# Two-layer decoder trunk: other places for the odd layer's decays, another order of its third head's projections, and other lengths in its list schedule

## The chip, the cores and the metric

The kernel runs on one core of one Trainium2 chip, as one launch. The metric is the device time of one execution in microseconds (us). An execution under the profiler gives the trace; its own time stands beside the times of runs without it.

## The reference, cut to what matters

One sequence of 1024 tokens with width 1024 goes through an even layer (windowed attention and a gated linear recurrence), an odd layer (gated DeltaNet) and a last RMSNorm. The change touches the odd layer alone, the last third of the kernel's instructions and some 1020 of its 2234 us. With 8 key heads of 128 and two value heads of 128 for each, it computes:

```python
def odd_mixer(hn, w_in, conv_w, dt_bias, a_log, norm_w, w_out):
    qkv, z, b_logit, a_logit = _split(hn @ w_in, ODD_SIZES)
    qkv = jax.nn.silu(causal_depthwise_conv(qkv, conv_w))
    q, k, v = _split(qkv, ...)          # q, k are l2-normalized
    beta = jax.nn.sigmoid(b_logit)
    g = -jnp.exp(a_log) * jax.nn.softplus(a_logit + dt_bias)
    o = gated_delta_rule_chunked(q, k, v, g, beta)
    o = rms_norm(o, norm_w) * jax.nn.silu(z)
    return o @ w_out

# gated_delta_rule_chunked, for one chunk, gcum = cumsum(g) within it
lower = where(strict, (k * beta) @ k.T * exp(gcum_i - gcum_j), 0)
u, w  = solve(I + lower, [v * beta, k * beta * exp(gcum)])
attn  = where(causal, q @ k.T * exp(gcum_i - gcum_j), 0)
v_new = u - w @ S
o     = (q * exp(gcum)) @ S + attn @ v_new
S     = S * exp(g_last) + (k * exp(g_last - gcum)).T @ v_new
```

The exponentials of differences of `gcum` are the decays: one 128 x 128 matrix for `lower` and one for `attn`, for every chunk and value head.

## The kernel before, in words

**Tiling.** The odd layer walks over the 8 key heads `hh`; both value heads (`e` = 0, 1) of a key head go together, so most tiles of the recurrence are 128 x 2 x 128. The sequence is cut into `NT` = 8 chunks `c` of 128 tokens. All projections are products of the normed input `hn` with weights in three fp32r terms (hi x hi, hi x lo, lo x hi), 128 x 512 a matmul: 8 slices of the inner dimension by 3 terms are 24 matmuls for one half of the tokens, 48 for one column group of 128. Their PSUM banks are `pj`, of which there are two (`BANKS`, L303).

**Stages for a head.** `proj(j)` (L1182) holds the column groups that are computed while an earlier head's recurrence runs: first `way_out(j - 2)` (the two groups of the gate z of head j - 2), then k of head j + 1, the two v groups and q of head j. PSUM names in the profile: `pk`, `pv`, `pq` for these, `oz` for z. `conv` (L1103) does the causal convolution and SiLU on ACT and DVE after a projection, `turn_k`, `turn_v`, `turn_q` transpose on PE. Weights come in units of two column groups: `unit` (L349) hands out the next one of `queue` (L316) and loads the one after it; each is four DMAs of 256 KB into `raww`, split by an ACT cast (hi) and a DVE subtraction (lo). The units are w41 (k0), w42 (k1, v0_0), w43 (v0_1, q0), w44 (k2, v1_0), w45 (v1_1, q1), w46 (z0), w47 (k3, v2_0), w48 (v2_1, q2) and so on.

**`invert(hh)`** (L1255) builds the inverse of I + `lower` for all 16 chunk and value-head pairs: `kk` = k k^T on PE; DVE multiplies it by beta and the decay into the big tile `L` (128 x 16 x 128, two places); then 31 steps on 32 x 32 blocks (`Lp`, `Tp`, `tm` on DVE) and small matmuls (`qp`, `up`, `q2`, `u2`) turn L into the inverse U, in the same tile. The decays come from `gcd`, a 128 x 128 array of `gcum` in DRAM that `gates()` (L1039) writes at the start of the layer: `decays` (L1249) loads two rows of it, the same for all partitions, into a small tile of 128 x 2 x 128 (128 KB of writes), and `decay_l` (L1261) runs two relus with a bias and one exponential on it. For L these tiles are `gcl` (two places, 8 loads a head), for the attention matrix `gca` (two places, 8 loads a head), which POOL masks and ACT exponentiates.

**`recur(hh)`** (L1360) is the recurrence over the chunks. A chunk is a chain between engines: `ks` = k S on PE, `r` on DVE, `vp` = U r on PE, `vt` on DVE and `vn` on ACT, `kv` = k^T vt on PE, then the new S on DVE. Beside it run `qs` (its eviction is `oq`, on ACT), `op` = A vn and `qk` for the next chunk; `attend` (L1372) multiplies `qk` with the decay into `A` (two places).

**The gate's way out.** `gate` (L1197) evicts `oz` into `g` (128 x 512, one place), for both e and both halves h: four tiles a head. `gated` multiplies the normed output by g and stores it to `ymix`; `normed` needs the whole recurrence of that head. At the end, `out_last` loads the mixed tiles back (`rawy`, cast into `oyh` and `yplo`) and the residual (`hr`, eight loads), multiplies by the output weights, adds and norms.

**What sets the order.** The code is written as generators, and `mix` and `blend` (L366, L376) interleave recurrence, inversion and projections by rough amounts of work. In the odd layer nothing is issued at once: each call is recorded by `Plan` and `run` (L203) makes a list schedule over all five engines. It simulates time with `times` (L107: how long an instruction holds its engine and when its result is there) and `SEM` (the delay of a semaphore to another engine), and takes on each engine, among the instructions that could start, the one that was recorded first. `give` (L266) then issues all in the order of the simulated starts, and each engine works strictly in that order. A tile whose place is still used waits for its old users. Since all of them go through one helper, the profile shows every instruction of the odd layer on L270 (and the even layer's on L284).

Of the kernel before, what the change touches and what calls it, by code (L numbers as in the profile page):

```python
# [10 lines left out]
F32 = mybir.dt.float32  # L11
# [70 lines left out]
class Plan:  # L82
# [7 lines left out]
    SEM = {"PE": 500, "DVE": 300, "ACT": 300, "POOL": 300, "SP": 300}  # L90

    def __init__(self):
        self.ops = None
# [13 lines left out]
    def times(self, op, last):  # L107

        key, name, a = op["key"], op["name"], op["a"]
        n = self.elems(op["out"][0])  # L110
        if key == "SP":
            return 420, 3200
        if key == "PE":
            if name == "transpose":
                return 109, 280
            r32 = a[1].dtype == F32R
            rows, cols = a[2].ap[0][1], self.elems(a[1])
            small = rows < 128 or cols < 128
            if small:
                held = 2.0 * (8 if cols == 32 else 18)  # L120
            else:
                held = n / 2.4 * (1 if r32 else 4) + (14 if r32 else 8)
            if small != last.get("small", False):
                held += 120
            last["small"] = small
            return held, held + 190
        if key == "DVE":
            if name == "transpose":
                t = 1950 if n >= 1024 else 1070 if op["out"][0].ap[-1][0] != 1 or a[1].ap[-1][0] != 1 else 620
            elif name == "memset":  # L130
                t = 60 + 0.82 * n
            elif n < 20:
                t = 85
            elif n >= 512:
                t = 100 + 1.15 * n
            else:
                t = 70 + 1.08 * n
            return t, t + 80
        if key == "ACT":
            t = 210 + 0.75 * n if n > 128 else 300  # L140
            if "accum_out" in op["kw"]:
                t = 440
            return t, t + 95
        if name == "memset":
            return 560, 600
        t = 780 if n <= 256 or a[0].ap[0][1] == 32 else 1330
        return t, t + 40
# [55 lines left out]
    def run(self):  # L203
# [42 lines left out]
        while done_n < n:  # L246
# [9 lines left out]
            i = min(i for i in ready[k] if at[i] <= s)  # L256
# [34 lines left out]
def trunk_kernel(ctx: ExitStack, tc: tile.TileContext, x, ew, ewo, ow, owab, owo, nw, fnw, lbl, hnw,  # L291
# [26 lines left out]
    for i in (21, *sorted(range(24), key=lambda i: (i // 3 + i % 3, i % 3 < 2, i) if i % 3 == 2 else (i // 3, 1, i))):  # L318
        queue += [(ow[i], 4)]
# [70 lines left out]
    def drain(fill):  # L390
        for _ in fill:
            pass
# [634 lines left out]
    def odd_layer(es):  # L1027
# [221 lines left out]
        def decays(hh, c, w):  # L1249
            g = sp.tile([P, 2, 128], F32, name=f"gc{w}{hh}_{c}", tag=f"gc{w}", bufs=2)  # L1250
# [4 lines left out]
        def invert(hh):  # L1255
# [5 lines left out]
            def decay_l(c):  # L1261
                gcB = decays(hh, c, "l")

                for e in range(2):
                    act.activation(gcB[:, e, :], gcB[:, e, :], AF.Relu, bias=gt["ngc"][:, c, 2 * hh + e:2 * hh + e + 1])
                act.activation(gcB, gcB, AF.Exp, scale=-1.0)
                return gcB

            ahead_l = [decay_l(0)]
            for h in range(2):  # L1270
# [4 lines left out]
                for c in range(4 * h, 4 * h + 4):  # L1275
                    gcB = ahead_l.pop()
                    if c < NT - 1:
                        ahead_l.append(decay_l(c + 1))
# [81 lines left out]
        def recur(hh):  # L1360
# [4 lines left out]
            def decay_a(c):  # L1365
                DA = decays(hh, c, "a")
# [5 lines left out]
            def attend(c):  # L1372
# [190 lines left out]
```

## Time and profile before

| | |
|---|---|
| median of 3 runs | 2235.93 us (2234.35 to 2236.56) |
| the profiled execution | 2235.39 us, of which its span is 2233.6 us |
| mean granted TensorE clock | 0.979 |
| HBM read, written | 151.25 MB, 29.49 MB |
| ACT / POOL busy | 947.2 us / 239.2 us |
| loads of L's decays (`gcl`) | 64 of 128 KB, 3.2 us from issue to landing |
| loads of A's decays (`gca`) | 64 of 128 KB, 3.0 us |
| loads of odd weights (`raww`) | 100 of 256 KB, 3.0 us |

Lines of operations give name and PSUM or SBUF tile as out<-in, partitions x elements, and a count; buffer numbers are left out, so `oz` is z of any head. PE is the matrix engine, PEld its weight load, DVE, ACT and POOL are the vector, scalar and GpSimd engines, SP issues the DMAs. A granted clock of 1.00 is TensorE's full speed, 0.50 half of it. The page cuts the span into 40 slices of 55.8 us with the busy tenths of each engine; the clock's row and PE's are:

```profile
PE   7999999999999999989998998899999999999998
PEclk9999999999999999989998998799999999999999
```

The 25th and 26th of them (1340 to 1452 us) are in the odd layer, where heads 0 and 1 are worked on.

### The profile page before, as it was taken

Reading aid. Unit: us, or ns where it says so; the run is one execution under the profiler, and the core shown is the slowest. Engines: PE = TensorE matmul, PEld = TensorE weight load, DVE = VectorE, ACT = ScalarE, POOL = GpSimd, SP = SyncE. Lnnn points to the kernel's source line nnn. Section 1 sums busy time; section 2 is a strip of 40 time slices with the busy share of each in tenths; the row PEclk is TensorE's granted clock in tenths of the full one; section 3 lists DMA queues with packets and bytes.
Section 4 is the critical chain, followed back from the end, with each engine's and each line's share of the span. In section 5 each row is a group of like instructions: output and inputs, shape, how many; then the busy total and the mean of one; then the engine's idle time right before and its main releaser. Section 6 shows DMA issues by size and latency. Waiting matters only on the chain. (4 is left out here: it accounts for less than half of the span.)

```text
span 2233.6 us, 52459 instructions
## 1 busy us (share of the span) xinstructions
PE 2162.9 (97%) x21781; PEld 1780.9 (80%) x21781; DVE 1393.5 (62%) x3236; ACT 947.2 (42%) x2551; POOL 239.2 (11%) x252
## 2 busy tenths in 40 slices
PE   7999999999999999989998998899999999999998
PEld 6888888888787878767786776788888888887886
DVE  6353545453444444446666798697897988865677
ACT  6233333333223222222124855657566565653223
POOL 0011111110000000000000001312212121130100
PEclk9999999999999999989998998799999999999999
DMA  4111111114333434362233212212213121224223
GB/s 149 39 49 45 48 44 49 49 39 122 84 102 93 114 104 115 92 171 88 92 100 108 87 46 55 70 48 79 79 57 83 49 83 53 83 74 150 89 95 123
DMA packets 100078, 184.14 MB, mean 82 GB/s; under 512 B 12672, under 2 KB 30208, under 8 KB 99840
## 3 DMA queue, kind: packets, MB, share of 16 engines
q1 hardware_dynamic: 99840, 180.79, 26.5%
q8 instruction: 171, 2.80, 0.5%
q14 instruction: 67, 0.55, 0.1%
HBM read 151.25 MB, written 29.49 MB: 81 GB/s over the span
## 5 line engine op out<-in xcount | busy, mean ns | idle before, releaser
L284 DVE TENSOR_TENSOR w_lo<-raww,w_hi 128x512 fp32r<-128x512 f32 x160 | 117.9, 740 | 150.0 <-ACT w_hi L284 149.5
L284 ACT CAST w_hi<-raww 128x512 fp32r<-128x512 f32 x160 | 99.4, 621 | 203.7 <-DMA raww<-in_ewo_dram 54.2
L270 PE MATMUL op<-w_hi,yplo 128*128 128x512 f32 x448 | 140.4, 392 | 0.7 <-DVE hr L270 0.6
L284 ACT ACTIVATE P<-P,nm 128x256 f32<-128x256 f32 (+7 forms) x128 | 71.4, 559 | 133.4 <-DVE nm L284 133.3
L270 ACT CAST w_hi<-raww 128x512 fp32r<-128x512 f32 x132 | 81.8, 621 | 89.8 <-DMA raww<-in_owo_dram 42.8
L270 DVE TENSOR_TENSOR hr<-hr,op 128x512 f32<-128x512 f32 x128 | 87.4, 685 | 48.7 <-PE op L270 46.2
L284 PE MATMUL op<-w_hi,yphi 128*128 128x512 f32 x320 | 105.9, 405 | 7.9 <-DVE hres L284 4.8
L270 DVE TENSOR_TENSOR w_lo<-raww,w_hi 128x512 fp32r<-128x512 f32 x132 | 96.3, 732 | 20.5 <-ACT w_hi L270 17.5
L270 PE MATMUL pv<-hn_hi,w_hi 128*128 128x512 f32 x256 | 107.4, 419 | 0.0
L270 PE MATMUL oz<-hn_hi,w_hi 128*128 128x512 f32 x256 | 107.3, 419 | 0.0
L270 PE MATMUL pv<-hn_hi,w_lo 128*128 128x512 f32 x256 | 103.6, 405 | 0.0
L270 PE MATMUL pv<-hn_lo,w_hi 128*128 128x512 f32 x256 | 102.4, 400 | 0.0
L270 PE MATMUL oz<-hn_hi,w_lo 128*128 128x512 f32 x256 | 102.2, 399 | 0.0
L270 PE MATMUL oz<-hn_lo,w_hi 128*128 128x512 f32 x256 | 101.9, 398 | 0.0
L284 DVE STREAM_TRANSPOSE PB<-P 128x256 f32<-128x256 f32 (+3 forms) x64 | 54.6, 853 | 72.9 <-ACT P L284 72.9
L270 PEld LDWEIGHTS op<-w_hi,yplo 128*128 128x128 f32 x448 | 84.1, 188 | 18.9 <-DVE hr L270 1.5
L270 POOL TENSOR_TENSOR gca<-gca,MA 128x256 f32<-128x256 f32 x64 | 54.6, 854 | 366.0 <-DMA gca<-gcd 196.3
L270 PE MATMUL op<-w_lo,yplo 128*128 128x512 f32 x224 | 86.9, 389 | 0.0
L284 DVE TENSOR_TENSOR hres<-hres,op 128x512 f32<-128x512 f32 x96 | 64.7, 682 | 31.7 <-PE op L284 30.9
L284 DVE CUSTOM_DVE_ANT_0 P<-S,G 128x256 f32<-128x256 f32 (+7 forms) x128 | 58.1, 491 | 36.8 <-PE S L284 36.5
L284 PEld LDWEIGHTS op<-w_hi,yphi 128*128 128x128 f32 x320 | 62.0, 194 | 23.8 <-DVE hres L284 5.6
L284 PE MATMUL avp<-w_hi,hn_hi 128*128 128x256 f32 x256 | 74.6, 291 | 0.0
(345 smaller groups left out, 6352.6 us busy)
## 6 DMA issues: line engine op xcount, KB each, us to landing
raww<-in_ew_dram SPq DMA_DIRECT2D x128, 256.0 KB, 3.0
raww<-in_ow_dram SPq DMA_DIRECT2D x100, 256.0 KB, 3.0
V<-vd SPq DMA_DIRECT2D x64, 256.0 KB, 5.3
rawy<-ymix SPq DMA_DIRECT2D x64, 256.0 KB, 2.7
raww<-in_ewo_dram SPq DMA_DIRECT2D x32, 256.0 KB, 3.0
gcl<-gcd SPq DMA_DIRECT2D x64, 128.0 KB, 3.2
gca<-gcd SPq DMA_DIRECT2D x64, 128.0 KB, 3.0
ymix<-oy SPq DMA_DIRECT2D x32, 256.0 KB, 2.8
```

Of the source, the lines that this page charges most:

```text
L270: ops[i]["f"](*ops[i]["a"], **ops[i]["kw"])
L284: return f(*a, **kw)
```

## The change

**Places of the decays.** `decays` no longer loads into tiles of its own. For L, `invert` loads two chunks (four matrices) at a time straight into their part of `L`, four DMAs of 256 KB a head instead of eight of 128 KB; ACT does four relus and one exponential on 512 elements there, and DVE multiplies in place. For A the load goes into a tile of tag `A`, which now has four places, and `attend` multiplies in place.

**Order.** `proj(2)`, the projections issued beside head 1's recurrence and ahead, no longer begins with the gate z of head 0: it is v2_0, then z0 with `GATE` = 8 steps of it ahead of k3, then the rest of z0, v2_1 and q2. The `queue` of weights follows: w46 is now (k3, v2_0) and w47 is z0. The gate's tile `g` has two places.

**The schedule.** Each recorded instruction gets a rank `want`, which is its number in the record, less `lead` for steps wrapped in `plan.early`: `gates()` and `invert(0)` are recorded with a lead of 10000. The list schedule takes the least `want` among what could start. `SEM` goes from 300 to 250 for four engines, an engine's wait for its own result from 0 to 40 (`OWN`), and most lengths in `times` are other numbers.

The diff, cut to its core (of the lengths two lines are shown):

```diff
-    SEM = {"PE": 500, "DVE": 300, "ACT": 300, "POOL": 300, "SP": 300}
+    SEM = {"PE": 500, "DVE": 250, "ACT": 250, "POOL": 250, "SP": 250}
+    OWN = 40
...
-        self.ops.append(dict(key=key, f=f, name=name, a=a, kw=kw, out=out, ins=ins, i=len(self.ops)))
+        self.ops.append(dict(key=key, f=f, name=name, a=a, kw=kw, out=out, ins=ins, i=len(self.ops), want=len(self.ops) - self.lead))
+    def early(self, lead, steps):
+        while True:
+            old, self.lead = self.lead, lead
+            z = next(steps, None)
+            self.lead = old
+            if z is None:
+                return
+            yield z
...
         if key == "SP":
-            return 420, 3200
+            return 430, 3100
...
-                if k is None or k == key and k not in ("PE", "SP"):
+                if k is None:
                     t = done
                 else:
-                    t = 0.0 if k == key == "PE" else done + self.SEM[k]
+                    t = 0.0 if k == key == "PE" else done + (self.OWN if k == key else self.SEM[k])
...
-            i = min(i for i in ready[k] if at[i] <= s)
+            i = min((i for i in ready[k] if at[i] <= s), key=lambda i: ops[i]["want"])
...
-    for i in (21, *sorted(range(24), key=lambda i: (i // 3 + i % 3, i % 3 < 2, i) if i % 3 == 2 else (i // 3, 1, i))):
+    for i in (21, *sorted(range(24), key=lambda i: (i // 3, 1, i) if i % 3 < 2 else (i // 3 + 2, i == 2, i + 4.5 * (i == 2)))):
...
         def proj(j):
-            if j > 1:
+            if j > 1 and j != 2:
                 yield from way_out(j - 2)
             w = unit()
             late = (lambda: turn_q(j - 1)) if j else (lambda: turn_k(0))
-            if j < 7:
-                yield from conv(w, 0, 9 + j, f"k{j + 1}", lambda: k_tile(j + 1), late)
-            yield from conv(w, 1, 16 + 2 * j, f"v{j}_0", lambda: v_tile(j, 0), (lambda: turn_k(j + 1)) if j < 7 else late)
+            k = lambda mid: conv(w, 0, 9 + j, f"k{j + 1}", lambda: k_tile(j + 1), mid)
+            v = lambda mid: conv(w, 1, 16 + 2 * j, f"v{j}_0", lambda: v_tile(j, 0), mid)
+            tk = lambda: turn_k(j + 1)
+            tv = lambda: turn_v(j, 0)
+            if j == 2:
+                yield from v(late)
+                out = way_out(0)
+                for _ in range(GATE):
+                    yield next(out)
+                yield from k(None)
+                yield from out
+                tv = lambda: (turn_v(j, 0), turn_k(j + 1))
+            elif j < 7:
+                yield from k(late)
+                yield from v(tk)
+            else:
+                yield from v(late)
             w = unit()
-            yield from conv(w, 0, 17 + 2 * j, f"v{j}_1", lambda: v_tile(j, 1), lambda: turn_v(j, 0))
+            yield from conv(w, 0, 17 + 2 * j, f"v{j}_1", lambda: v_tile(j, 1), tv)
             yield from conv(w, 1, j, f"q{j}", lambda: q_tile(j), lambda: turn_v(j, 1))
+        GATE = 8
...
-                g = G7[0][:, e, h, :] if hh == 7 else sp.tile([P, 512], F32, name=f"g{hh}_{e}_{h}", tag="g")
+                g = G7[0][:, e, h, :] if hh == 7 else sp.tile([P, 512], F32, name=f"g{hh}_{e}_{h}", tag="g", bufs=2)
...
-        def decays(hh, c, w):
-            g = sp.tile([P, 2, 128], F32, name=f"gc{w}{hh}_{c}", tag=f"gc{w}", bufs=2)
+        def decays(hh, c):
+            g = sp.tile([P, 2, 128], F32, name=f"A{hh}_{c}", tag="A", bufs=4)
...
-            def decay_l(c):
-                gcB = decays(hh, c, "l")
-                for e in range(2):
-                    act.activation(gcB[:, e, :], gcB[:, e, :], AF.Relu, bias=gt["ngc"][:, c, 2 * hh + e:2 * hh + e + 1])
-                act.activation(gcB, gcB, AF.Exp, scale=-1.0)
-                return gcB
-            ahead_l = [decay_l(0)]
+            for c in range(0, NT, 2):
+                sync.dma_start(L[:, 2 * c:2 * c + 4, :],
+                               bass.AP(tensor=gcd.tensor, offset=gcd.offset + (c * 16 + 2 * hh) * 128,
+                                       ap=[[0, P], [16 * 128, 2], [1, 256]]))
+                for u in range(4):
+                    act.activation(L[:, 2 * c + u, :], L[:, 2 * c + u, :], AF.Relu,
+                                   bias=gt["ngc"][:, c + u // 2, 2 * hh + u % 2:2 * hh + u % 2 + 1])
+                act.activation(L[:, 2 * c:2 * c + 4, :], L[:, 2 * c:2 * c + 4, :], AF.Exp, scale=-1.0)
...
                         dve.scalar_tensor_tensor(L[:, 2 * c + e, :], kk[:, c - 4 * h, :], SC[hh][:, 0, c, e:e + 1],
-                                                 gcB[:, e, :], op0=ALU.mult, op1=ALU.mult)
+                                                 L[:, 2 * c + e, :], op0=ALU.mult, op1=ALU.mult)
...
-                A = sp.tile([P, 2, 128], F32, name=f"A{hh}_{c}", tag="A", bufs=2)
-                dve.tensor_tensor(A, qk[:, None, :].to_broadcast([P, 2, 128]), DA, op=ALU.mult)
-                return A
+                dve.tensor_tensor(DA, qk[:, None, :].to_broadcast([P, 2, 128]), DA, op=ALU.mult)
+                return DA
...
-        fill = blend(gates(), start())
+        fill = blend(plan.early(10000, gates()), start())
...
-        drain(blend(invert(0), fill, 0.8))
+        drain(blend(plan.early(10000, invert(0)), fill, 0.8))
```

What that makes of the order on each engine is shown at three places. A row has the line, the operation and out<-in with the tiles' full names (the head and the chunk stand behind the letters: `ks0_5` is chunk 5 of head 0, `oz0_0_0` the first half of z0's first column group).

First PE, where head 0's recurrence is at chunk 5. Before:

```order
L270 MATMUL ks0_5_14593<-S0_4_14584,kT0_14256 128x256
L270 MATMUL qs0_5_14595<-S0_4_14584,q0_14392 128x256
L270 MATMUL vp0_5_14600<-r0_5_14594,L0_14294 128x128 x2
L270 MATMUL op0_5_14606<-vn0_5_14602,A0_5_14588 128x128
L270 MATMUL kv0_5_14604<-vt0_5_14601,kn0_14292 128x256
L270 MATMUL op0_5_14606<-vn0_5_14602,A0_5_14588 128x128
L270 MATMUL qk0_6_14608<-q0_14392,kT0_14256 128x128
L270 MATMUL ks0_6_14612<-S0_5_14605,kT0_14256 128x256
L270 MATMUL qs0_6_14614<-S0_5_14605,q0_14392 128x256
```

With the change:

```order
L291 MATMUL oz0_0_0_14675<-hn_hi0_13908,w47_hi0_14616 128x512
L291 MATMUL ks0_5_14571<-S0_4_14563,kT0_14256 128x256
L291 MATMUL qs0_5_14573<-S0_4_14563,q0_14384 128x256
L291 MATMUL oz0_0_0_14675<-hn_lo0_13910,w47_hi0_14616 128x512
L291 MATMUL oz0_0_0_14675<-hn_hi0_13908,w47_lo0_14617 128x512
L291 MATMUL oz0_0_0_14675<-hn_hi1_13909,w47_hi1_14619 128x512
L291 MATMUL oz0_0_0_14675<-hn_lo1_13911,w47_hi1_14619 128x512
L291 MATMUL oz0_0_0_14675<-hn_hi1_13909,w47_lo1_14620 128x512
L291 MATMUL oz0_0_0_14675<-hn_hi1_13909,w47_hi1_14619 128x512
L291 MATMUL oz0_0_0_14675<-hn_lo1_13911,w47_hi1_14619 128x512
L291 MATMUL oz0_0_0_14675<-hn_hi1_13909,w47_lo1_14620 128x512
L291 MATMUL vp0_5_14578<-r0_5_14572,L0_14294 128x128
```

Before, the chunks 4 to 7 of head 0 follow each other on PE with no projection between them. Now matmuls of z0 stand between the steps of a chunk, eight of them between `qs0_5` and the first `vp0_5`.

Second SP, which issues the loads, where the array `gcd` has just been written. Before:

```order
L270 DMA gcd_14213<-gcs__14227 128x128
L270 DMA gcl0_0_14296<-gcd_14213 128x256
L270 DMA gcl0_1_14298<-gcd_14213 128x256
L270 DMA gca0_0_14395<-gcd_14213 128x256
L270 DMA raww44_0_14328<-in_ow_dram 128x512
L270 DMA gca0_1_14418<-gcd_14213 128x256
L270 DMA raww44_1_14331<-in_ow_dram 128x512
L270 DMA gcl0_2_14299<-gcd_14213 128x256
L270 DMA gcl0_3_14300<-gcd_14213 128x256
```

With the change:

```order
L291 DMA gcd_14213<-gcs__14227 128x128
L291 DMA raww43_2_14268<-in_ow_dram 128x512
L291 DMA raww43_3_14271<-in_ow_dram 128x512
L291 DMA L0_14294<-gcd_14213 128x2x256 x4
L291 DMA A0_0_14387<-gcd_14213 128x256
L291 DMA L1_14388<-gcd_14213 128x2x256 x4
L291 DMA raww44_0_14320<-in_ow_dram 128x512
L291 DMA raww44_1_14323<-in_ow_dram 128x512
```

Before, single loads of decays stood among those of the weights w44. Now the eight loads of L for heads 0 and 1, with A's first between them, are in one piece ahead of w44.

Third ACT, near the end of the layer, where `rawy` is cast into `yplo` and chunk 5 of head 7 follows. Before:

```order
L270 CAST yplo1_9_16379<-rawy256_0_1_16381 128x512
L270 ACTIVATE oj7_4_0_16403,oss7_16242<-bv7_16197 128x128
L270 CAST yplo1_9_16379<-rawy256_1_0_16382 128x512
L270 ACTIVATE oj7_4_1_16404,oss7_16242<-bv7_16197 128x128
L270 CAST yplo1_9_16379<-rawy256_1_1_16383 128x512
L270 ACTIVATE oq7_5_16410<-qs7_5_16409,g_eg_14220 128x128 x2
```

With the change:

```order
L291 CAST yplo1_9_16254<-rawy256_0_1_16256 128x512
L291 ACTIVATE oj7_4_0_16277,oss7_16122<-bv7_16079 128x128
L291 ACTIVATE oj7_4_1_16278,oss7_16122<-bv7_16079 128x128
L291 CAST yplo1_9_16254<-rawy256_1_0_16257 128x512
L291 CAST yplo1_9_16254<-rawy256_1_1_16258 128x512
L291 ACTIVATE oq7_5_16284<-qs7_5_16283,g_eg_14220 128x128 x2
```

Two squares (`oj7_4`) stand in another place between the casts; `oq7_5` is behind the last cast in both.

More of the change, by code (lines that the diff above doesn't have):

```diff
@@ L119, in times @@
             if small:
-                held = 2.0 * (8 if cols == 32 else 18)
+                held = 28 if cols == 32 else 62
             else:
-                held = n / 2.4 * (1 if r32 else 4) + (14 if r32 else 8)
+                held = n / 2.4 * (1 if r32 else 4) + (17 if r32 else 8)
             if small != last.get("small", False):
-                held += 120
+                held += 100
             last["small"] = small
@@ L128, in times @@
             if name == "transpose":
-                t = 1950 if n >= 1024 else 1070 if op["out"][0].ap[-1][0] != 1 or a[1].ap[-1][0] != 1 else 620
+                t = 1980 if n >= 1024 else 1060 if out.ap[-1][0] != 1 or a[1].ap[-1][0] != 1 else 95 + 1.03 * n
             elif name == "memset":
-                t = 60 + 0.82 * n
-            elif n < 20:
-                t = 85
+                t = 60 + 0.86 * n
+            elif n < 24:
+                t = 82
+            elif out.ap[0][1] == 32:
+                t = 715
             elif n >= 512:
-                t = 100 + 1.15 * n
-            else:
-                t = 70 + 1.08 * n
-            return t, t + 80
+                t = (65 if name == "scalar_tensor_tensor" and len(op["ins"]) == 3 else 12) + 1.155 * n
+            elif name == "scalar_tensor_tensor":
+                t = 260
+            else:
+                t = 72 + 1.03 * n
+            return t, t + 83
         if key == "ACT":
[L140 to L143, printed above, removed]
+            if n < 24:
+                t = 200
+            elif op["ins"][0].space == PSUM:
+                t = 249 if n <= 128 else 268 if n <= 256 else 0.93 * n
+            else:
+                t = 293 if n <= 128 else 307 if n <= 256 else 1.02 * n
+            if n >= 512 and (len(op["ins"]) > 1 or out.ap[0][1] == 32):
+                t += 100
+            return t, t + (230 if "accum_out" in op["kw"] else 110)
         if name == "memset":
-            return 560, 600
-        t = 780 if n <= 256 or a[0].ap[0][1] == 32 else 1330
-        return t, t + 40
+            return 565, 565
+        t = 750 if n <= 256 or out.ap[0][1] == 32 else 1010 if len(op["ins"][1].ap) > 2 else 1250
+        return t, t + 50
     def edges(self):
```

14 lines of the change are left out of this document (6 added, 8 removed).

## The prediction

> **What bounds the kernel now.** I read the page first, then the busy time by stage, then what TensorE (PE) waited for, then its timeline where it waited longest.
>
> ```profile
> span 2233.6 us, 52459 instructions
> ...
> PE 2162.9 (97%) x21781; PEld 1780.9 (80%) x21781; DVE 1393.5 (62%) x3236; ACT 947.2 (42%) x2551; POOL 239.2 (11%) x252
> ```
>
> PE is busy for 97% of the span, so an edit pays only where PE idles or runs at a lower clock. The odd layer begins near 1213 us. The next rows are the busy time in stretches of it: stretch, length, then PE, PE's weight loads, DVE, ACT, POOL with instruction counts, and last the granted clock, DMA share and rate.
>
> ```profile
> 1250.00:1275.00 25.00, 21.42 (x97) 17.28 (x96) 19.60 (x58) 18.93 (x58) 2.08 (x2) 0.93 0.33 98
> 1275.00:1350.00 75.00, 73.96 (x555) 60.51 (x554) 67.95 (x172) 40.95 (x107) 5.89 (x9) 1.00 0.19 57
> 1350.00:1368.78 18.78, 18.78 (x99) 16.04 (x97) 14.61 (x36) 15.03 (x46) 2.62 (x3) 1.00 0.37 88
> 1368.78:1419.76 50.98, 38.71 (x335) 30.32 (x334) 36.27 (x124) 18.36 (x61) 13.59 (x18) 0.60 0.09 26
> 1419.76:1507.00 87.24, 85.97 (x633) 71.48 (x632) 73.65 (x214) 56.78 (x174) 13.50 (x17) 1.00 0.23 66
> 1507.00:2020.00 513.00, 512.24 (x3621) 427.95 (x3621) 417.57 (x1129) 311.28 (x943) 118.26 (x127) 1.00 0.25 72
> 2020.00:2060.00 40.00, 35.51 (x159) 29.24 (x158) 20.68 (x44) 12.77 (x37) 1.61 (x2) 0.91 0.48 172
> 1450.00:1500.00 50.00, 50.00 (x413) 41.61 (x412) 48.41 (x140) 30.05 (x87) 8.03 (x10) 1.00 0.14 41
> ```
>
> The loss sits in one place: from 1368.78 to 1419.76 PE is idle for 50.98 - 38.71 = 12.3 us and its clock is 0.60. From 1507 to 2020, heads 2 to 6, it is idle for 0.8 of 513 us at full clock: nothing is to be won there. What that stretch looks like, in PE's timeline (start, length, operation, in brackets the idle time before and who ended it), first where chunks of head 0's recurrence stand among projection matmuls, then where they stand alone:
>
> ```profile
> 1361.65 0.48 PE L270 MATMUL oz<-hn_hi,w_hi 128*128 128x512 f32 x1
> 1361.97 0.59 PE L270 MATMUL kv<-vt,kn 128*128 128x256 f32 x2
> 1362.40 0.38 PE L270 MATMUL qk<-q,kT 128*128 128x128 f32 x2
> 1362.54 0.47 PE L270 MATMUL oz<-hn_lo,w_hi 128*128 128x512 f32 x1
> ...
> 1364.24 0.60 PE L270 MATMUL ks<-S,kT 128*128 128x256 f32 x2
> 1364.67 0.59 PE L270 MATMUL qs<-S,q 128*128 128x256 f32 x2
> ...
> 1365.34 0.40 PE L270 MATMUL oz<-hn_hi,w_hi 128*128 128x512 f32 x1
> 1365.57 0.40 PE L270 MATMUL oz<-hn_lo,w_hi 128*128 128x512 f32 x1
> ```
>
> ```profile
> 1372.27 0.67 PE L270 MATMUL ks<-S,kT 128*128 128x256 f32 x2 [0.82 <-DVE tm L270]
> ...
> 1378.43 0.95 PE L270 MATMUL ks<-S,kT 128*128 128x256 f32 x2 [1.00 <-DVE S L270]
> 1379.17 1.06 PE L270 MATMUL qs<-S,q 128*128 128x256 f32 x2
> 1381.01 1.22 PE L270 MATMUL vp<-r,L 128*128 128x128 f32 x4 [0.78 <-ACT oq L270]
> 1382.75 0.80 PE L270 MATMUL op<-vn,A 128*128 128x128 f32 x2 [0.52 <-ACT vn L270]
> 1383.34 1.09 PE L270 MATMUL kv<-vt,kn 128*128 128x256 f32 x2
> ...
> 1385.42 1.19 PE L270 MATMUL ks<-S,kT 128*128 128x256 f32 x2
> ```
>
> From start to start a projection matmul takes 0.23 us (1365.34 to 1365.57), a pair on 128x256 0.43 (kv to qk, ks to qs), so a pair on 128x128 about half, 0.22. A chunk is three pairs of the first kind (ks, qs, kv) and five of the second (two vp, two op, qk): 1.29 + 1.10 = 2.4 us of PE. Alone it takes 1378.43 - 1372.27 = 6.2 us, since each step waits for DVE or ACT, and 1385.42 - 1378.43 = 7.0 us once the clock is halved. The projection that should lie between is out of work: oz of head 0 has one place for its gate g, and the place comes free only when head 0's recurrence is over and its output is normed.
>
> **The change part by part**, against the profiled execution's own 2235.39 us (span 2233.6 and 1.8 around it); the median of the three runs is 0.5 above that.
>
> *Order of the third head's projections, and two places for g.* Nothing is added or removed. In the changed PE order, from ks of chunk 3 of head 0 on, 15 to 23 matmuls of pv2, oz0 and pk3 stand between one ks and the next (91 in all), where before 16 stood in chunk 3 and none in chunks 4 to 7. A chunk needs 6.2 - 2.4 = 3.8 us of cover; 18 matmuls of 0.23 are 4.1. The cover is there, not by much. What goes is what the stretch wastes. From below: PE's busy time at the granted clock is at most 38.71 x 0.60 = 23.2 us of full-speed work, so at least 50.98 - 23.2 = 27.8 us are lost. From above: if all of it is stretched like a chunk, 2.4 of 7.0, the work is 17.5 us and 33.5 are lost. Both rows describe the same stretch, so I take the middle, **-31**.
>
> *What is late next: DVE.* From 1275 to 1507 DVE is busy for 67.95 + 14.61 + 36.27 + 73.65 = 192.5 of 232 us, and its work stays. Were it to reach the share of 1275 to 1350 (67.95 / 75 = 0.906), it would need 212.5 us, and only 19.5 could be saved; at the share of 1450 to 1500 (48.41 / 50 = 0.968) 198.8 us, and 33 could. I take what lies between, nearer the upper row because that one has PE at 50.00 of 50: 28 saved, that is **+3** on the term above.
>
> *Decays loaded into L's and A's own places.* Each head loads L in four DMAs of 256 KB instead of eight of 128 KB, with one exponential on 512 columns where two on 256 stood: 32 DMAs and 32 ACT instructions fewer. ACT and SP bound nothing (56.78 of 87.24 busy on ACT at the busiest), so I cost that at nothing; the cover is PE's own work. But in SP's changed order the loads for L of heads 0 and 1 stand in one piece, with A's first between them, ahead of the weights w44. How fast such loads run, before, is in the SP queue's timeline and the DMA rate by slices of 0.275 us from 1246 to 1257:
>
> ```profile
> 1246.89 0.80 SPq L270 DMA_DIRECT2D gcl<-gcd  x2
> 1247.74 0.43 SPq L270 DMA_DIRECT2D gca<-gcd  x1
> 1248.27 0.38 SPq L270 DMA_DIRECT2D raww<-in_ow_dram  x1
> ```
>
> ```profile
> GB/s 205 22 0 0 0 0 26 89 89 93 71 93 89 93 71 71 52 97 115 97 89 134 253 294 175 164 186 190 179 175 264 257 197 205 89 86 93 74 37 7
> ```
>
> While gcl and gca alone are in flight the rate is about 90 GB/s. At that rate a load of L takes 2.9 us, four 11.6, and all nine some 25 us: L0 is whole about 10 us after its first load, and the weights behind it land near 1270 instead of 1255. ACT and DVE take their work in order, so PSUM copies and weight splits behind L0's exponentials wait too. PE before loses there:
>
> ```profile
> PE kk L270 <- DVE L L270: 2.8, 1, 2.8
> ```
>
> That wait may go, since gates and inversion now come first (by some 2 us at PE), or be replaced by one for the copies behind L. Bounds: 3.6 us better (all of 25 - 21.42) and 9 worse (the 11.6 less the 2.8 waited now). I take **+3**, nearer the middle since the first PE work that needs w44 (pk2) stands over 20 us behind.
>
> The Trainium skill ("DMA: Bandwidth & Descriptors", Anatomy of one DMA) fits a DMA at about 2.0 us plus its bytes at 436 GB/s, for the GpSimd path; by that, an estimate, a load of L costs 2.6 us, mostly latency that overlaps, and the four land within 4 us of one another. The rate row disagrees for these loads, which read the same few rows for all partitions; by the page the last term would be nothing and the time 2207.
>
> *List schedule with new lengths.* It orders all of the layer. Where PE is at 512.24 of 513 there is nothing to win: 0, with 5 us either way as many ranks change. The stall near 2041 to 2046 stays:
>
> ```profile
> 2043.89 0.62 ACT L270 CAST yplo<-rawy 128x512 fp32r<-128x512 f32 x1 [6.83 <-DMA rawy<-ymix]
> ```
>
> The cast waits for a load that stands in SP's queue behind eight loads of the residual, and the changed order has the same eight ahead of it and the same oq behind it. Nothing of the 40 - 35.51 is won.
>
> **Sum:** -31 + 3 + 3 = -25 us: 2235.4 - 25 = **2210 us**.
>
> **Rivals.** *DVE is the bound* (chance 0.16). It gets through its work no faster than at 0.906: 19.5 saved, less 3 for L, gives 2219. For it: from 1275 to 1350 it is the fullest engine beside PE. Against it: 48.41 of 50 later on. *All of it goes* (0.13): 33 saved and the early wait gone too gives 2199. *The stall only moves* (0.04): PE's filling is used up early and PE starves later instead, from 1420 to 1507; 2235. Against it: PE would have to lose 25 us where it is now idle for 1.3, with both orders alike again from head 2's recurrence on.
>
> *Slower* (0.04): the burst of L loads in every head. Each L now has to wait for its place, then for 11.6 us of loads, and ACT, in order, holds PSUM copies behind its exponentials. PE has two banks for projections, 24 matmuls or 5.5 us each; once ACT is held for longer, PE stops. It decides from there on. A stop of the size seen at 2041 (4.5 idle, and 0.91 of the clock over 40 us adds some 3) is about 7 us; in each of seven heads that is 49, less 25: 2259. Against it is what ACT waits now between 1500 and 2000, without PE noticing:
>
> ```profile
> ACT gcl L270 <- DMA gcl<-gcd: 23.0, 17, 4.1
> ```
>
> *The clock does not come back* (0.01). The stretch has a clock of 0.60 though the idle times before its rows are 1.0 us or less; if something else halves it, only the 12.3 idle us can go: 2223. The Trainium skill ("TensorE: Matmul & The Clock Gate", HAM oscillation) gives the rule that only PE-idle gaps over about 3.4 us matter. The trace speaks against that as a rule on single gaps, since short ones in a row were enough here; and the clock is 1.00 again as soon as projections return.
>
> **How the numbers follow.** The forecast has 0.62, for 2203 to 2217: DVE's bounds, L's from -3 to +9 and the 5 us either way do not add up all in one direction. With the two neighbours the range is **2199 to 2222**, which leaves out the same, the slower and a little at both ends. A change of 0.2%, 4.5 us, is about what a measurement of this kernel can tell from none. Faster by more than that: 0.62 + 0.16 + 0.13 + 0.01 = **0.92**; the same **0.04**; slower **0.04**.
>
> **What would show it.** Right: no PE stretch with a clock of 0.6 between head 0's chunks 3 and 7; oz and pk between ks and vp there; DVE at 0.93 or more of the time from Lp0 to head 2's first chunk; the 4.5 us stop near the end unchanged. For L: loads of L0 that land about 3 us apart. Wrong: PE waits for ACT behind L's exponentials in each head, or a new stretch at half clock in heads 1 or 2.

## The result, and the profile after

The changed kernel takes 2266.55 us (median of 4 runs, 2264.51 to 2271.7) against 2235.14 of the kernel before beside it: ratio 1.0143, 95% interval 1.0125 to 1.0162. It is slower by 31 us, where 25 less were predicted. The profiled execution took 2265.53 us. First its page (span, then busy time of each engine):

```profile
span 2263.8 us, 52378 instructions
...
PE 2159.7 (95%) x21781; PEld 1777.9 (79%) x21781; DVE 1410.1 (62%) x3236; ACT 943.2 (42%) x2519; POOL 240.7 (11%) x252
```

PE does the same matmuls and is idle for 2263.8 - 2159.7 = 104.1 us, before for 70.7. Busy time by stretch of the changed kernel, with the columns and the bounds of the prediction's table:

```profile
1250.00:1275.00 25.00, 19.81 (x85) 16.04 (x84) 17.18 (x47) 18.65 (x55) 3.31 (x4) 0.86 0.46 106
1368.78:1419.76 50.98, 42.32 (x400) 34.26 (x400) 31.87 (x95) 26.96 (x76) 14.39 (x17) 0.90 0.25 48
1419.76:1507.00 87.24, 75.63 (x580) 61.68 (x579) 71.93 (x210) 50.00 (x150) 19.65 (x22) 0.94 0.31 73
1507.00:2020.00 513.00, 486.88 (x3451) 406.69 (x3451) 421.64 (x1100) 287.70 (x855) 105.90 (x115) 0.98 0.21 64
```

The stretch that was to get better did: from 1368.78 the clock is 0.90 where it was 0.60, and 8.7 us are idle, not 12.3. Head 0's chunks are covered as forecast: PE is not idle there until 1390, when L's loads for head 2 go out. The 8.7 us come behind these: 5.5 at `ot` (transposes of the output `bv`), which waits for POOL, which waits for a load of A until 1407.83, and 3.2 at `q`, which waits for a step of the inversion that stands behind the relus on ACT. At the first head, from 1250 to 1275, 5.2 us are idle where 3.6 were. The loss is where nothing had been lost: 11.6 us idle from 1419.76 (1.3 before) and 26.1 from 1507 to 2020 (0.8 before), with a clock that falls below 1. What PE waits for in the odd layer (total, times, longest):

```profile
PE kk L291 <- DVE L L291: 30.2, 12, 6.6
PE up L291 <- issue: 8.4, 1, 8.4
PE ot L291 <- POOL bv L291: 5.5, 1, 5.5
PE q L291 <- ACT L L291: 4.1, 2, 3.2
```

The first row is new in size: before it stood at 2.8 in one place. The page's part on DMA issues (count, size, median us from issue to landing) says what is behind it:

```profile
L<-gcd SPq DMA_DIRECT2D x32, 256.0 KB, 11.7
A<-gcd SPq DMA_DIRECT2D x64, 128.0 KB, 2.9
```

A load for L lands after 11.7 us; the small loads of before took 3.2, and the list schedule plans 3.1. A load of A that goes out behind such a burst is late too, up to 15.6 us where the median is 2.9. One of the stops, in head 4, by the timelines of SP, ACT, DVE and PE (in brackets the idle time before, and who ended it):

```profile
1583.46 1.92 SPq L291 DMA_DIRECT2D L<-gcd  x4
...
1589.16 0.69 ACT L291 ACTIVATE L<-L,g_ngc 128x128 f32<-128x128 f32 x2 [2.80 <-DMA L<-gcd]
...
1597.93 0.40 ACT L291 ACTIVATE L<-L,g_ngc 128x128 f32<-128x128 f32 x1 [3.58 <-DMA L<-gcd]
...
1599.05 0.61 ACT L291 ACTIVATE uq<-q 128x512 f32<-128x512 f32 x1
...
1599.70 0.69 DVE L291 SCALAR_TENSOR_TENSOR q<-uq,q 128x512 f32<-128x512 f32 x1 [4.17 <-ACT uq L291]
1600.31 0.34 DVE L291 SCALAR_TENSOR_TENSOR L<-kk,sc,L 128x128 f32<-128x128 f32 x1
...
1594.22 0.83 PE L291 MATMUL kk<-kT 128*128 128x128 f32 x6
1600.71 0.80 PE L291 MATMUL kk<-kT 128*128 128x128 f32 x2 [5.65 <-DVE L L291]
1601.15 0.77 PE L291 MATMUL oz<-hn_hi,w_hi 128*128 128x512 f32 x1
1601.73 0.63 PE L291 MATMUL oz<-hn_lo,w_hi 128*128 128x512 f32 x1
1602.15 0.63 PE L291 MATMUL oz<-hn_hi,w_lo 128*128 128x512 f32 x1
```

The four loads go out at once when L's place is free. ACT, in order, stands at a relu until the third lands (1597.93); behind it is `uq`, a step of the convolution of q. DVE waits for that, and its first multiplication into L is behind. PE waits 5.65 us for that multiplication at the last of the four products of `kk`, and then runs at half speed for some 3 us more (0.42 from start to start where 0.23 is full speed). The same chain comes back in heads 5, 6 and 7 (4.9, 6.7 and 5.1 us).

### The profile page after: what moved, and what is told of

Its sections match the earlier page's. It is cut to its first block, busy times and chain, and to the rows that moved or that the text cites. A ratio compares the mean times of both kernels' runs of the same rounds, so it can differ in the third digit from the quotient of the medians.

```text
span 2263.8 us, 52378 instructions
## 1 busy us (share of the span) xinstructions
PE 2159.7 (95%) x21781; PEld 1777.9 (79%) x21781; DVE 1410.1 (62%) x3236; ACT 943.2 (42%) x2519; POOL 240.7 (11%) x252
## 5 line engine op out<-in xcount | busy, mean ns | idle before, releaser
L291 POOL TENSOR_TENSOR A<-A,MA 128x256 f32<-128x256 f32 x64 | 53.4, 836 | 447.7 <-DMA A<-gcd 217.5
L291 DVE SCALAR_TENSOR_TENSOR vT<-uv,cws,vT 128x512 f32<-128x512 f32 x96 | 73.7, 769 | 4.6 <-ACT vT L291 2.9
## 6 DMA issues: line engine op xcount, KB each, us to landing
L<-gcd SPq DMA_DIRECT2D x32, 256.0 KB, 11.7
```

Of the source, the lines that this page charges most:

```text
L291: ops[i]["f"](*ops[i]["a"], **ops[i]["kw"])
```

## The experiments

All were measured with runs of the kernel before on the same chip (its medians there: 2232.8 to 2234.3). A table first; "rows" is the order of the decays' array in DRAM, explained below.

| kernel | loads for L | order of head 2's projections | plan | median us | ratio to before, interval |
|---|---|---|---|---|---|
| e1_small_loads | 8 small, apart | new | new | 2227.5 | 0.9973 (0.9963 to 0.9984) |
| e2_in_place_only | 4 in L | old | old | 2272.3 | 1.0169 (1.0149 to 1.0189) |
| e3_order_only | 8 small, apart | new | old | 2228.2 | 0.9974 (0.9964 to 0.9984) |
| e4_long_l_in_plan | 4 in L | new | new, L's load long | 2221.9 | 0.9941 (0.9923 to 0.9958) |
| e5_one_run_rows | 4 in L, new rows | new | new | 2213.1 | 0.9907 (0.989 to 0.9923) |
| e6_one_run_rows_plan | 4 in L, new rows | new | new, L's load measured | 2210.0 | 0.9901 (0.9886 to 0.9915) |
| e7_long_l_old_order | 4 in L | old | new, L's load long | 2225.1 | 0.9968 (0.9957 to 0.9979) |
| e8_lengths_only | 8 small, apart | old | new | 2239.9 | 1.0032 (1.002 to 1.0044) |
| e9_rows_plan_old_order | 4 in L, new rows | old | new, L's load measured | 2226.0 | 0.9966 (0.9953 to 0.9979) |
| e10_rows_in_place_only | 4 in L, new rows | old | old | 2234.6 | 1.0009 (1.0 to 1.0019) |
| e11_rows_in_place_order | 4 in L, new rows | new | old | 2226.3 | 0.9968 (0.9955 to 0.9981) |

**Which part costs: e1 to e4.** The changed kernel with the small loads back (`oy` gives up a place for their tiles):

```diff
-            for c in range(0, NT, 2):
-                sync.dma_start(L[:, 2 * c:2 * c + 4, :],
-                               bass.AP(tensor=gcd.tensor, offset=gcd.offset + (c * 16 + 2 * hh) * 128,
-                                       ap=[[0, P], [16 * 128, 2], [1, 256]]))
+            def decay_l(c):
+                gcB = decays(hh, c, "gcl", 2)
...
-            y = sp.tile([P, 512], F32, name=f"oy{hh}_{e}_{h}", tag="oy", bufs=2)
+            y = sp.tile([P, 512], F32, name=f"oy{hh}_{e}_{h}", tag="oy")
```

> The changed kernel, but the decays for L are loaded as before: eight loads of 128 KB a head into two small tiles, two ahead (the tile oy has one place instead of two, to make room). All else is the change's: the order of the third head's projections, two places for g, A in place, the new lengths. Theory 'burst' (the four loads of L at once hold the DMA engines for 15 us in each head; ACT, DVE and then PE at kk wait behind them): the stops of heads 2 to 7, some 55 us of the trace's excess, go, and 2205 to 2218 us come out, no PE wait for kk over 1 us in heads 4 to 7. Theory 'schedule' (the new lengths put kk too early on PE, however the decays are loaded): 2250 or more. Theory 'order' (the moved projections upset the later heads): 2250 or more.

2227.5: the slowdown is gone and 'schedule' and 'order' fall, but the gain is 7 us, not the 16 to 29 that 'burst' had. What PE waits for longest from 1340 to 1600 in the profiled execution, which was its slowest (2233.95 us):

```profile
PE qp L291 <- DVE ors L291: 5.0, 1, 5.0
PE qp L291 <- DVE Un L291: 2.9, 1, 2.9
```

At `kk` it waits 0.4 us at the longest there and 1.2 in the later heads. PE waits at `qp` for DVE, which ends the inversions of heads 1 and 2 too late.

The kernel before with L and A in place and nothing else:

```diff
-                gcB = decays(hh, c, "l")
...
+            for c in range(0, NT, 2):
+                sync.dma_start(L[:, 2 * c:2 * c + 4, :],
+                               bass.AP(tensor=gcd.tensor, offset=gcd.offset + (c * 16 + 2 * hh) * 128,
+                                       ap=[[0, P], [16 * 128, 2], [1, 256]]))
```

> The kernel before with one part of the change: decays loaded into L (four loads of 256 KB) and into A (four places). Order, g and lengths are those of before. Theory 'burst': stops in most heads as in the changed kernel, some 40 to 55 us, so 2270 to 2295 us, with the bare stretch of head 0 still at half clock. Theories 'schedule' and 'order': within 6 us of before.

2272.3, as 'burst' said: this part alone costs 38 us. The other theories had it at no difference; they fall. Here PE stops at other places than in the changed kernel: at `qk` for DVE's work on q, which in head 5 waits for `uq` behind a relu on ACT (13.2 us in 5 places), and at `ot` for POOL's `bv` (11.4 in 6). The order alone:

```diff
-            if j > 1:
+            if j > 1 and j != 2:
                 yield from way_out(j - 2)
...
-                g = G7[0][:, e, h, :] if hh == 7 else sp.tile([P, 512], F32, name=f"g{hh}_{e}_{h}", tag="g")
+                g = G7[0][:, e, h, :] if hh == 7 else sp.tile([P, 512], F32, name=f"g{hh}_{e}_{h}", tag="g", bufs=2)
...
-            y = sp.tile([P, 512], F32, name=f"oy{hh}_{e}_{h}", tag="oy", bufs=2)
+            y = sp.tile([P, 512], F32, name=f"oy{hh}_{e}_{h}", tag="oy")
```

> The kernel before with the other part of the change alone: the third head's projections and their weights in the new order and two places for g (oy has one place instead of two, to make room). Decays and lengths are those of before. Theory 'burst': the prediction's first two terms were right, 2206 to 2216 us, and no stretch at half clock between 1370 and 1420 us. Theory 'order': 2235 or more.

2228.2, a miss for both theories: the order gains 6 us, not 18 to 28. Its windows show where the rest went:

```profile
1350.00:1368.78 18.78, 14.80 (x81) 12.51 (x81) 12.71 (x33) 15.86 (x59) 1.74 (x2) 0.94 0.27 57
1368.78:1419.76 50.98, 50.32 (x411) 41.55 (x411) 47.20 (x135) 25.57 (x73) 14.01 (x16) 0.96 0.15 44
...
1450.00:1475.00 25.00, 22.43 (x103) 17.45 (x102) 24.71 (x84) 16.26 (x54) 2.70 (x3) 0.86 0.11 29
1475.00:1507.00 32.00, 28.88 (x291) 22.79 (x290) 26.39 (x71) 10.88 (x28) 10.79 (x13) 0.95 0.23 67
...
1507.00:1600.00 93.00, 88.73 (x668) 73.02 (x669) 77.57 (x223) 58.47 (x179) 14.51 (x17) 1.00 0.20 62
```

The old stretch is full (50.32 of 50.98). But PE now loses 4.0 us just ahead of it, where it lost none: 3.5 of them at `vp` for `oq`, on ACT, which is busy for 15.86 of 18.78. And it loses 2.6 + 3.1 + 4.3 us from 1450 to 1600, most of it in waits for DVE, which from 1450 to 1475 is busy for 24.71 of 25: it is behind with head 2's inversion. The one place of `oy` is no part of this: ACT waited for it 0.2 us in all. Then the changed kernel, with the plan told of longer loads:

```diff
-            return 430, 3100
+            return (3600, 6000) if n == 512 and op["ins"][0].ap[0][0] == 0 else (430, 3100)
```

> The changed kernel with one number of the list schedule changed: a load of L is planned as 3.6 us on its queue and 6.0 us to its landing, where 0.43 and 3.1 were planned, so that the last of four lands 17 us after the first begins. The loads themselves are the same. Theory 'burst', if the harm is that the plan does not know how long they take: ACT's and DVE's work is placed ahead of the relus, kk later, most of the stops of heads 4 to 7 (31 us) go, 2215 to 2240 us. If the harm is in the DMA engines themselves (other loads and what else moves through them stand behind the burst, whatever the order): 2250 or more. Theory 'schedule' would also have this one within 10 us of the changed kernel.

2221.9, 45 us below the changed kernel with the same loads: most of the harm was that the plan did not know their length. The loads land hardly sooner (9.7 us in the median), but in head 4 ACT now does `uq` before the relus of the second load, and ACT's waits for L's loads from 1500 to 2000 fall from 27.0 us to 4.6. From 1340 to 1600 one long stop is left:

```profile
PE up L291 <- issue: 10.2, 1, 10.2
PE u L291 <- issue: 2.2, 1, 2.2
PE kk L291 <- DVE L L291: 2.0, 4, 0.7
```

"issue" means that PE waited for nothing the profile shows. The changed kernel has the same in the middle of the `up` matmuls of head 2, while L's loads for head 3 are in flight; PE's timeline, then the DMA queues over 1460 to 1491 and over 1491 to 1494:

```profile
1494.28 0.26 PE L291 MATMUL up<-Q,Tn 32*32 32x32 f32 x2 [8.39 <-issue]
...
q1 hardware_dynamic: 1697, 1.92, 44.0%
q14 instruction: 2, 0.02, 0.2%
...
q1 hardware_dynamic: 508, 0.78, 74.6%
q8 instruction: 1, 0.02, 1.9%
```

Queue 8 carries instruction code; for which engine, the profile does not say. It moved nothing from 1460 to 1491, one packet after that, and PE went on at 1494.28. So PE most likely waited for its code, which stood behind L's loads. This is read from the order in time; no kernel moved the code's loads alone.

**How the load's time comes about: e5 and e6.** The decays of one head lie 16 rows apart in the array, so that a load of two chunks reads two runs of 1 KB for each partition. The rows were put in the order head, chunk, value head, so that it reads one run of 2 KB:

```diff
+            gp = cs[:, 3, :]
+            dve.tensor_copy(gp.rearrange("p (h c e) -> p h c e", h=8, e=2), gt["gc"].rearrange("p c (h e) -> p h c e", e=2))
-            pe.transpose(tq, gt["gc"].rearrange("p c h -> p (c h)"), ident)
+            pe.transpose(tq, gp, ident)
...
-                               bass.AP(tensor=gcd.tensor, offset=gcd.offset + (c * 16 + 2 * hh) * 128,
-                                       ap=[[0, P], [16 * 128, 2], [1, 256]]))
+                               bass.AP(tensor=gcd.tensor, offset=gcd.offset + (hh * 16 + 2 * c) * 128,
+                                       ap=[[0, P], [128, 4], [1, 128]]))
```

> The changed kernel with the array of decays in DRAM written in another order (head, chunk, value head instead of chunk, head, value head; one small DVE copy more at the start of the layer), so that each load of L reads one run of 2 KB a partition instead of two of 1 KB. Bytes, DMAs and the plan's lengths are the change's. Theory 'packets' (a load's time goes by the number of its packets): the four loads land some 7 us after the first begins instead of 15, the stops in heads 2 to 7 shrink by about half or more, 2225 to 2245 us. Theory 'bytes' (it goes by the bytes, or by all partitions reading one row): landing stays at 14 to 15 us, 2260 or more.

2213.1: 53 us less than the changed kernel, by the order of rows alone (51 with each taken against the kernel before beside it). That is outside both ranges, on the side of 'packets': the loads got shorter by more than the number of their packets, which halved. The loads' line on its page:

```profile
L<-gcd SPq DMA_DIRECT2D x32, 256.0 KB, 4.6
```

While L's loads are in flight in head 5, the changed kernel (10 us in slices of 0.25) has this busy share of 16 DMA engines, in tenths, and this rate:

```profile
DMA  3443444342220222120122122002212211131221
GB/s 86 90 86 78 90 94 90 70 90 53 86 90 16 86 86 90 53 66 0 70 90 82 61 90 86 0 0 86 90 53 86 90 66 74 49 131 49 90 90 57
```

and e5_one_run_rows in head 4 (5 us in slices of 0.125):

```profile
DMA  8674572764756799999997999998886544322500
GB/s 311 246 246 180 148 131 82 164 147 131 197 147 197 262 328 377 328 393 344 426 361 295 344 336 352 360 393 320 320 295 246 197 164 172 123 66 74 172 0 0
```

With 1-KB runs about a quarter of the engines is at work here and 90 GB/s is all there is; with 2-KB runs nine tenths are, and over 300 GB/s at best. The 90 GB/s do not come from the jump between a load's two runs: the small loads of before read a single run of 1 KB and moved at the same rate. The Trainium skill ("DMA: Bandwidth & Descriptors", Specifications) puts the smallest transfer for line rate at 512 B; 1 KB is above that, so the measurement differs from it here. With the plan told 1.8 us on the queue and 4.5 to the landing:

```diff
-            return 430, 3100
+            return (1800, 4500) if n == 512 and op["ins"][0].ap[0][0] == 0 else (430, 3100)
```

> e5_one_run_rows, and the list schedule plans a load of L as 1.8 us on its queue and 4.5 us to its landing. Theory 'packets': loads and plan agree, PE's stop of 10 us within the up matmuls of head 2 that e4_long_l_in_plan still has goes with the burst, 2205 to 2216 us, below before and near the time that was predicted. Theory 'bytes': 2220 to 2240 us, no better than e4_long_l_in_plan.

2210.0, the lowest median of all; PE's wait at `up` is 0.5 us, in e5 2.6. The 3 us to e5_one_run_rows are within the spread of the two (2208.3 to 2212.6 here, 2208.8 to 2213.2 there), so with short loads no gain from telling the plan is shown. That this is the predicted time is chance: it is another kernel, and its terms are not those of the prediction.

**What the order and the plan are worth: e7 to e11.** In e7 and e9 the order goes back:

```diff
-            if j > 1 and j != 2:
+            if j > 1:
                 yield from way_out(j - 2)
...
-                g = G7[0][:, e, h, :] if hh == 7 else sp.tile([P, 512], F32, name=f"g{hh}_{e}_{h}", tag="g", bufs=2)
+                g = G7[0][:, e, h, :] if hh == 7 else sp.tile([P, 512], F32, name=f"g{hh}_{e}_{h}", tag="g")
```

> e4_long_l_in_plan with the third head's projections, their weights and the one place for g as before. It tells what the order is worth beside decays that are in place and planned at their length. Theory 'DVE is free earlier' (with all decays of L ready at once, the inversions of heads 1 and 2 are done earlier, so that DVE no longer holds PE up later and the order gains what was predicted): 2240 to 2250 us, 18 to 28 above e4_long_l_in_plan, with the bare stretch of head 0 at half clock back. Theory 'the order only moves the stall', as e3_order_only seemed to say: 2225 to 2232 us.

2225.1, at the edge of what the second theory had. But e4_long_l_in_plan holds the stop of 10.2 us that e7 has not, so the two were compared again without a burst:

> e6_one_run_rows_plan with the third head's projections, their weights and the one place for g as before. With no burst in either, it tells what the order is worth. Theory 'the order gains what was predicted once L's decays come at once': 2228 to 2236 us, 18 to 26 above e6_one_run_rows_plan. Theory 'the order moves most of the stall' (e7_long_l_old_order came out only 3 above e4_long_l_in_plan): 2212 to 2220 us.

2226.0, 16 us above e6_one_run_rows_plan, between the theories and nearer to the first. The windows, first e9 and then e6:

```profile
1350.00:1420.00 70.00, 61.17 (x472) 50.11 (x471) 53.92 (x165) 37.13 (x111) 18.94 (x23) 0.80 0.19 60
1420.00:1507.00 87.00, 85.56 (x630) 70.63 (x629) 78.16 (x209) 53.42 (x163) 19.50 (x21) 1.00 0.21 64
1507.00:1600.00 93.00, 92.06 (x672) 77.01 (x671) 80.49 (x211) 56.81 (x171) 19.74 (x21) 1.00 0.22 69
```

```profile
1350.00:1420.00 70.00, 69.56 (x563) 58.33 (x562) 60.02 (x174) 46.55 (x140) 18.52 (x22) 1.00 0.20 63
1420.00:1507.00 87.00, 84.67 (x638) 69.57 (x637) 78.70 (x239) 52.59 (x158) 24.26 (x26) 1.00 0.25 81
1507.00:1600.00 93.00, 90.77 (x664) 75.30 (x662) 80.65 (x215) 56.64 (x168) 19.28 (x21) 1.00 0.21 65
```

With the order, PE's 8.8 idle us and the clock of 0.80 go from the first stretch, and some 2 us more are idle in the next two. The plan's part alone, on the kernel before:

```diff
-    SEM = {"PE": 500, "DVE": 300, "ACT": 300, "POOL": 300, "SP": 300}
+    SEM = {"PE": 500, "DVE": 250, "ACT": 250, "POOL": 250, "SP": 250}
+    OWN = 40
...
-        fill = blend(gates(), start())
+        fill = blend(plan.early(10000, gates()), start())
```

> The kernel before with the list schedule's part of the change alone: the new lengths, semaphore delays, ranks and the lead of gates and the first inversion. Loads, places and the order of the projections are those of before. The prediction's term for it was 0, 5 us either way: 2230 to 2240 us. Theory 'schedule' (it is the lengths that hurt): 2245 or more.

2239.9 against 2233.0 beside it: 7 us slower, at the edge of what was expected and a little beyond the prediction's 5; 'schedule' falls. Alone, then, the three parts give 38 (e2), -6 (e3) and 7 us (e8), 39 in all; together they gave 31. Last, the kernels with the old plan and the new rows, without the order and with it:

```diff
+            dve.tensor_copy(gp.rearrange("p (h c e) -> p h c e", h=8, e=2), gt["gc"].rearrange("p c (h e) -> p h c e", e=2))
...
+                sync.dma_start(L[:, 2 * c:2 * c + 4, :],
+                               bass.AP(tensor=gcd.tensor, offset=gcd.offset + (hh * 16 + 2 * c) * 128,
+                                       ap=[[0, P], [128, 4], [1, 128]]))
```

> e2_in_place_only (the kernel before with decays in L's and A's places, nothing else) with the decays' array in the new order of rows. Theory 'packets': the 38 us that e2_in_place_only lost against before are those of the burst, and 2222 to 2238 us come out. If more than half of the loss stays (2253 or more), it is the wait for L's place, not the load, that costs.

2234.6, as 'packets' said: decays in place cost nothing once the loads are short (38 us with the old rows), so the wait for L's place by itself is not what hurt. And with the order:

```diff
-            if j > 1:
+            if j > 1 and j != 2:
                 yield from way_out(j - 2)
```

> e10_rows_in_place_only with the third head's projections in the new order and two places for g, and the lengths of before. Theory 'DVE': in e3_order_only the multiplications into L are paced by two small tiles over 20 us, the inversions of heads 1 and 2 end late and PE waits for DVE from 1450 to 1570 us; with all decays at once that goes, and 2208 to 2218 us come out. Theory 'the order moves most of the stall, whatever the loads': within 7 us of e10_rows_in_place_only.

2226.3: 8 us below e10, a miss for both theories, and nearer to the second. With the old plan the order gains 6 to 8 us with either kind of load; only with the new plan does it gain 16. So the pace of the small tiles, which e11's expectation blamed for DVE being late in e3, is at most a part of it, and why the two need each other was not followed further.

## Why the prediction was wrong, step by step

- *What bounds the kernel*: right. The loss was where head 0's chunks stood alone, and with the new order most of it goes there (e3: 50.32 of 50.98 us busy; e6: 69.56 of 70 at 1.00).
- *Order, -31, and DVE late next, +3*: direction right, size not. Alone it gave -6 (e3), because PE then waited for DVE, which took 24.71 of 25 us at 1450, and lost 4.0 us to ACT just before the stretch, which no term had. The rival 'DVE is the bound' had this at 19.5 saved; even that was too much, since only the stretch to 1507 was counted, and DVE was late until 1600. With the other parts done well it gave -16.
- *Decays in L's and A's own places, +3*: **the step that failed.** The rate of 90 GB/s and the 25 us for nine loads were read rightly, and the bursts are of the size computed (11.6 us for four loads; they land after 5.3 to 16.9 us, 11.7 in the median, those of L0 about 3 us apart as said). At the first head the price held: 5.2 us idle where 3.6 were. But it was bounded at the first head alone, between 3.6 better and 9 worse, when such a burst comes in every head, and "the cover is PE's own work" left out that ACT, DVE and POOL stand behind it in order and then hold PE. The term measured 38 us alone (e2 against the kernel before) and 53 in the change (against e5).
- *The slower rival* had the mechanism: L waits for its place, then 11.6 us of loads; ACT, in order, holds PE's inputs; about 7 us a head; 2259. In the changed kernel PE stopped at `kk`, behind DVE, for 4.9 to 6.7 us in heads 4 to 7, and not at the banks of the projections. It was given 0.04, on the evidence of what ACT waited in the kernel before, 23.0 us from 1500 to 2000. That row came from loads of 128 KB that go out two ahead, before L's place is needed. And its sum is the wrong thing to look at: in the changed kernel ACT waits 27.0 us there, little more, and PE stops all the same, because of what stands behind the waiting relus in ACT's order.
- *List schedule, 0 and 5 either way*: it was costed as ranks that change. That its one length for every DMA, 3.1 us, would be wrong by a factor of four for the new loads was left out, though both numbers were at hand, 3.1 in the diff and 11.6 in the prediction; telling it was worth 45 us (e4 against the changed kernel). The other new numbers cost 7 us by themselves (e8).
- *The stall near the end* stayed, as said: PE waits 4.1 us at `vp` for `oq` in the changed kernel, later only because all is later. *The clock* in head 0's stretch came back, 0.90 in the changed kernel and 1.00 in e6, where e9, which differs in the order alone, has 0.80: so it was the bare chunks that held it down. The prediction's idle times of 1.0 us or less are those up to about 1400, and the clock had fallen by 1380; later in the stretch there are 1.4 and 2.2 us.

## What to carry to other kernels

When a transfer is moved into the place that will hold its result, it can start only when that place is free: unless the order of the work allows for its whole duration, engines wait for it in each round, so price it there and multiply by the rounds. A planner that gives every DMA one length has to be told when a load's size or its runs change, since engines that work in order can turn one load that is late into a stop of several. And look at the runs that a load reads before giving it up: here putting rows side by side took 53 us off the changed kernel, twice what the change was to win.

## What the runs showed of the hardware

- Loads of the same bytes, from the same few rows to 128 partitions, moved at about 90 GB/s in 1-KB runs and at 300 to 390 GB/s, at best, in 2-KB runs. By the rows above a busy engine moved the same in both, about 90 / (0.25 x 16) = 22 and 345 / (0.95 x 16) = 23 GB/s. But idle engines are not the cause: in head 3's burst, with other loads queued behind it, the engines are busy all the time from 1484 to 1487, and the rate is 77 GB/s. What sets this limit for the short runs is open.
- PE stopped for 8 to 10 us in the middle of a group of matmuls with no wait that the profile shows; its code seems to have been late behind a burst of loads. The Trainium skill ("Runtime: NRT & Kernel Launch", Instruction fetch mechanics) has code come in blocks of 16 KiB by a DMA queue of the engine's own and calls the cost mostly hidden. The size agrees (queue 8: 171 packets, 2.80 MB). If it was code that PE waited for, it was not hidden: 8.4 and 10.2 us in two kernels, 2.6 in e5 and 0.5 in e6, whose bursts are shorter.
- A single stop of 5.65 us brought half speed for some 3 us behind it, so that stop cost about 1.5 us more than its idle time.
